# mLSTM output stage: the products over 128 rows of all heads ahead of those over 64 rows, and four vectors of a filler step in one row

## The chip, the core and the metric

The kernel runs on one core of a Trainium2 chip, as one launch. The metric is device time in microseconds (us). Inside the core five engines work on queues of their own: TensorE (PE: matrix products, with PEld for its weight loads), VectorE (DVE), ScalarE (ACT), GpSimd (POOL) and SyncE (SP, which issues most of the transfers). TensorE reads its weights from a part of its 128 x 128 array; a product over 64 rows uses the upper or the lower half of the rows, a product with 32 columns of weights uses a strip of 32 columns.

## The reference, cut to what matters

One layer: a token mixer (bidirectional mLSTM with 4 heads, and a convolution group), then a mixture of 64 experts. The change lies in the mLSTM outputs and in the adaLN rows that are made beside them. For each chunk of 128 tokens, each direction and head:

```python
s = jnp.einsum('bhctk,bhcsk->bhcts', qc, kc) * jnp.exp(log_d - m_t[..., None])
e_int = jnp.exp(a - m_t)
num = (jnp.einsum('bhcts,bhcsv->bhctv', s, vc)
       + e_int[..., None] * jnp.einsum('bhcvk,bhctk->bhctv', C_prev, qc))
den = jnp.sum(s, axis=-1) + e_int * jnp.einsum('bhck,bhctk->bhct', n_prev, qc)
h = num / jnp.maximum(jnp.abs(den), jnp.exp(-m_t))[..., None]
```

The first sum runs over the 128 tokens of the chunk, the second over the 64 features of a head (QK_DIM = 64). The values have 128 features, and a column of ones makes the denominators along with them (129 columns). The adaLN rows are `silu(c) @ w_ada + b_ada`.

## The kernel before, in words

After the front (projections, gates, states of the chunks) `outputs` (L590 to L718) runs over 8 chunks x of 128 tokens. For each chunk and each direction d it makes
- `decay` (L617): the logarithms of the weights in `pM` by two products (L620, L623), their exponentials `Dm` on ScalarE (L626);
- `scores` (L613): four products over 64 rows (heads 0 and 2 in the lower half of the rows, 1 and 3 in the upper) into `pQ`; `scaled` (L633, L636): the scaled queries `qs`; and `Dm` times the scores (L645);
- `sums` (L649): for each head a product over 128 rows, `Dm` with the values `va` (L654), and a product over 64 rows, `qs` with the state `C` of tile `cst` (L655), added up in `pN`. There is one buffer of `pN`, two banks of PSUM; head h is in bank h % 2;
- `divide` (L660 to L667): ScalarE copies `pN` to `hd`, VectorE divides; then `norm`, and `gate` with four transposes (L685).

`sums` is called 16 times, so it has 64 products over 128 rows and 64 over 64 rows. Chunk x + 1 is prepared while chunk x is summed.

Between these, `filler(2)` takes two steps of `ada` (L721) twice in every chunk, 32 steps in all. A step loads two tiles of 256 KB each (`wa2`, five buffers, L750) and makes four products with 32 columns of weights (L753) into four strips of `pa`. The first 16 steps also load and split the output projection's weights (`wor`, L759).

A product of L613, L654, L655 or L753 runs in two passes on TensorE and stands as x2 in the trace; one of L633 or L685 has one pass. A scheduler sets the order in which each engine gets its instructions: it takes what it holds ready, in the priority of the program, so filler products stand wherever it put them. After the stage come the output projection (L436 to L438), the router, and the experts, whose weights SyncE streams in (L1423).

```python
            for h, p in heads:
                o = pN[:, h % 2, h // 2, :DV + 1]
                mm(o, Dm[:, h % 2, h // 2], va[:, x + 2, h], start=True, stop=False)
                mm(o, qs[p, h // 2], C[p, h // 2], start=False, stop=True)
```

Of the kernel before, what the change touches and what calls it, by code (L numbers as in the profile page):

```python
# [32 lines left out]
class Layer:  # L33
# [19 lines left out]
    # ---------------------------------------------------------------- constants  # L53
# [51 lines left out]
    # ---------------------------------------------------------------- front  # L105
    def front(self, cp):
# [27 lines left out]
        # ---- adaLN: shift and scale of the mixer, features on partitions  # L134
# [12 lines left out]
        def squares(src, a, b):  # L147
            """Sums of squares over tiles of features, for tokens a to b."""
            for k in range(8):
                sq = vf[:, NT * (1 + k % 3):][:, :b - a] if k else vf[:, a:b]  # L150
                nc.scalar.activation(sq, src[:, k], AF.Square)
                if k:
                    nc.vector.tensor_tensor(vf[:, a:b], vf[:, a:b], sq, op=OP.add)
# [21 lines left out]
        def products(k):  # L175
            """Shift and gain of the features of tile k, the input's features summed in four parts."""
            p, n = (small, 1) if k % 3 == 2 else (wl, 2)
            w = p.tile([128, 8, 256], F32, name="wa1", bufs=n)
            self.wa1 = nc.sync.dma_start(w, A["wa1"][k]).ins
            a1 = pa[:, k % 2]  # L180
            for i in range(2):
                for n in range(4):
                    mm(a1[32 * n:32 * n + 32], cs[:, 2 * n + i], w[:, 2 * n + i], start=i == 0, stop=i == 1,
                       skip_group_check=True)
# [50 lines left out]
        # The first products go along with the features.  # L235
        U, Y = X[:, :4], X[:, 4:]
        first = [(f, j, pj.tile([128, 512], F32, name="pf", bufs=4)) for j in range(2) for f in (8, 4)]
        # The tensor engine's clock is up only after work: products that nobody reads until the sums are there.
# [47 lines left out]
        # ---- projections with features on partitions  # L286
# [41 lines left out]
        # ---- values and gates with tokens on partitions  # L328
# [80 lines left out]
    def behind(self, engine=mybir.EngineType.PE):  # L409
        """What follows runs behind what the engine has been given so far."""  # L410
        return self.tc.issue_after(next(i for i in reversed(self.nc.cur_bb.bb.instructions) if i.engine == engine))

    @contextmanager
    def later(self, n):
        """Lower priority for the scheduler: work that fills gaps."""
        tc = self.tc
        tc.cur_priority += n
        yield
        tc.cur_priority -= n
# [20 lines left out]
    # ---------------------------------------------------------------- mLSTM  # L440
    def gates(self, sp, pp, gt, colG, colF, colW, acol):
        """In steps: other products come between them."""
# [89 lines left out]
    def bound_rows(self, cp):  # L532
        """-M and exp(m - M) as rows of all heads, one for every direction and chunk: the high parts and, at partition
        64, the low ones."""
        nc = self.nc
        sp, sp_ = self.pool("rwt", 1)
        self.idr = cp.tile([80, 16], F32R, name="idr")
        idf = sp.tile([80, 16], F32, name="idf")
        nc.vector.memset(idf, 0.0)
        for h in range(2):  # L540
            nc.vector.tensor_copy(idf[64 * h:64 * h + 16], self.ident[64 * h:64 * h + 16, 64 * h:64 * h + 16])
        nc.vector.tensor_copy(self.idr, idf)
        out = []
        for i in range(2):
            raw = sp.tile([80, 2, 256], F32, name=f"rw{i}")
            nc.vector.memset(raw, 0.0)
            for d in range(2):
                v = self.rowd[i, BWD * d + 8:BWD * d + 40].rearrange("(c a s) t -> s c a t", a=2, s=2)
                for p in (8 * d, 64 + 8 * d):
                    for s in range(2):  # L550
                        nc.sync.dma_start(raw[p:p + 8, s].rearrange("p (a t) -> p a t", a=2), v[s])
            R = cp.tile([80, 2, 256], F32R, name=f"rwR{i}")
            nc.scalar.copy(R, raw)
            nc.vector.tensor_tensor(R[64:], raw[64:], R[64:].bitcast(F32), op=OP.subtract)
            out.append(R)
        self.close(sp_)
        return out

    def states(self, sp, pp, va, kT, cst, colW, acol):
        """The states before each latent chunk."""  # L560
# [29 lines left out]
    def outputs(self, qT, kT, va, cst, colG, colF, rows, os):  # L590
# [48 lines left out]
        def products(x, Dm):  # L639
            """The weights within the chunk and the scaled queries, both ways."""  # L640
# [8 lines left out]
        def sums(x, d, Dm, qs):  # L649
            pN = pp.tile([128, 2, 2, 256], F32, name="pN")  # L650
            C = cst[:, d, x if d == 0 else 7 - x]
            for h, p in heads:
                o = pN[:, h % 2, h // 2, :DV + 1]
                mm(o, Dm[:, h % 2, h // 2], va[:, x + 2, h], start=True, stop=False)  # L654
                mm(o, qs[p, h // 2], C[p, h // 2], start=False, stop=True)  # L655
# [64 lines left out]
    # ---------------------------------------------------------------- adaLN of the later stages  # L720
    def ada(self, pp):  # L721
        """Gates, shift and scale as rows in DRAM; row j is made at partitions 32 j .. 32 j + 31."""
# [21 lines left out]
        for step in range(32):  # L744
            n, k = divmod(step, 8)
            if k == 0:
                ps = pp.tile([128, 256], F32, name="pa")
            for h in range(2):
                w = ap.tile([128, 2, 256], F32, name="wa2", bufs=5)
                nc.sync.dma_start(w, A["wa2"][n, k, :, 2 * h:2 * h + 2])  # L750
                for i in range(2):
                    j = 2 * h + i
                    nc.tensor.matmul(ps[32 * j:32 * j + 32], self.csil[:, k, 0:1].to_broadcast([128, 32]), w[:, i],  # L753
                                     start=k == 0, stop=k == 7, skip_group_check=True)
# [78 lines left out]
def cut(r):  # L833
    """Blocks of the expert with rank r: (first half of its list, rows). Those of 64 or 32 rows take native products
    and come first."""
# [7 lines left out]
def schedule():  # L843
    """Order of the experts (by rank)."""
# [12 lines left out]
def table():  # L857
    """Blocks in their order: (number of the expert, first half of its list, rows, column in the tables of rows).
    The shared expert comes first and last; its blocks are token tiles."""
# [23 lines left out]
class Full(Layer):  # L883
# [72 lines left out]
    # ---------------------------------------------------------------- token mixer output, router  # L956
    def mixer_out(self, cp, X):
# [111 lines left out]
        def place(j, pl, mask, eq):  # L1069
            """Place of every assignment in its expert's list: half block and row. The row's one-hot carries the  # L1070
            token's index in two parts."""
# [64 lines left out]
    def rms_apply(self, tp, v, g, add, junk, t, out, nm, eng=None):  # L1136
        """out = v rsqrt(mean v^2) g + add."""
# [9 lines left out]
    # ---------------------------------------------------------------- lists of the experts' tokens  # L1147
    def ranks(self, rp, bank, first_r, first_c):
        """Tokens of every expert and its rank by them, with experts on partitions (twice)."""
# [15 lines left out]
    def lead(self, cp, rp, pp):  # L1165
        """Some experts with a middling number of tokens so far take the first ranks: their weights are loaded ahead of
        the lists."""
# [17 lines left out]
    def route(self, cp, rp, pp, pI):  # L1185
        """Token and destination of every row of the half blocks, in the order of the static schedule."""
# [35 lines left out]
        # rows of the sums in parts, for the blocks of 64 and 32 rows  # L1222
# [5 lines left out]
        # blocks behind the schedule  # L1228
# [15 lines left out]
    def spill(self):  # L1244
        """Blocks of experts that have more tokens than the static schedule holds."""
# [95 lines left out]
    def row_weight(self, junk, x, e, out):  # L1341
        """Weight of expert e (its number in every row) in the rows of x."""
# [4 lines left out]
    def compact(self, rp, sl, width, outs, eq):  # L1347
        """sl (128, 8, 64): the slot of every (token, expert); outs: [(values (128, 64), psum (128 slots, blocks))]."""
# [23 lines left out]
    # ---------------------------------------------------------------- experts  # L1372
# [19 lines left out]
    def bank(self, name, *shape):  # L1392
        """A bank of PSUM for one of the four stages, from the two pools in turn."""
# [5 lines left out]
    def unit(self, dt, free, since, n=NU, keep=0):  # L1399
        """The unit that has been free for the longest time, or none if no more than keep of them are."""  # L1400
# [64 lines left out]
    def mm6(self, out, x, w, k, nk, s):  # L1465
        """out += x @ w."""
# [5 lines left out]
    def stage_gu(self, x, w, rows=128, rw=None):  # L1472
        """A block of 64 rows has up and gate in the two halves of the partitions, one of 32 rows also the two halves
        of the sum over the features. The rows' weights go with up."""
# [48 lines left out]
    def stage_dn(self, hT, w, b):  # L1523
        """Output rows, in two or four parts on top of each other for a block of 64 or 32 rows."""
# [14 lines left out]
        else:  # L1539
            n = 1  # L1540
# [20 lines left out]
    def pipeline(self, experts):  # L1561
        """experts in order of first use; the shared one (None) comes first and last."""
# [66 lines left out]
        def row(key):  # L1629
            """Half of a unit that holds a tile until the end."""  # L1630
# [6 lines left out]
        def run(i0, i1):  # L1637
            """The blocks i0 .. i1 - 1, one stage of each behind another's."""
# [54 lines left out]
    # ---------------------------------------------------------------- shared expert, sum over the chosen experts  # L1693
# [90 lines left out]
def layout():  # L1784
    """Tables of the static schedule: they depend on the shapes alone."""
# [22 lines left out]
```

## Time and profile before

| | us |
|---|---|
| median of 3 runs | 1513.09 (1513.04 to 1519.22) |
| profiled execution, first to last instruction (span) | 1511.1 |
| TensorE busy in the span | 1442.5 (95%) |
| VectorE, ScalarE, GpSimd busy | 1130.7, 754.4, 469.9 |
| TensorE's mean granted clock | 0.99 of 2.4 GHz |
| mean transfer rate | 246 GB/s |

The output stage runs from 326 us to about 434 us in the span. A row of the timeline gives start, length, engine, line, operation, the tile written and the tiles read, the part of the array (rows * columns), the shape, and the number of merged instructions. The length of a row of products reaches to the end of its last product; the next row can begin earlier, so the time that a row costs is read from start to start.

### The profile page before, as it was taken

The page shows a single profiled execution, that of the slowest core. Times are in us where ns is not written, and L with a number is a line of the kernel's source. Part 1 is how long each engine was busy: PE and PEld are TensorE (multiplying, and loading weights), DVE is VectorE, ACT ScalarE, POOL GpSimd, SP SyncE. Part 2 cuts the span into 40 slices and gives each one's busy share as a digit, 9 for nine tenths or more (in the row PEclk, how much of TensorE's full clock was granted, in tenths as well). Part 3 has the DMA queues.
Part 4 walks back from the last instruction along what each step waited for, and adds up shares of the span by engine and source line. Part 5 has one row for each costly group of instructions (what it writes and reads, how often), then busy time and mean ns, then how long its engine had stood idle before and what let it go on. Part 6 is the DMA issues. An engine that isn't in the chain of part 4 may idle for free. (4 is left out here: it accounts for less than half of the span.)

```text
span 1511.1 us, 22956 instructions
## 1 busy us (share of the span) xinstructions
PE 1442.5 (95%) x8205; PEld 1096.4 (73%) x8211; DVE 1130.7 (75%) x1942; ACT 754.4 (50%) x1241; POOL 469.9 (31%) x306
## 2 busy tenths in 40 slices
PE   6997999999999999999999999999999999999975
PEld 4787987765567754776788888888777777777764
DVE  6899979765657887843588788888777877777636
ACT  4420021244424335644566667677666776676621
POOL 0341101202112332233333323333433444555324
PEclk9999999999999999999999999999999999999998
DMA  8420051036544367998799999999999999999975
GB/s 334 158 77 28 1 196 31 18 111 220 171 155 164 142 242 283 334 329 283 247 287 323 328 314 326 328 341 343 322 352 285 348 331 305 313 351 322 335 249 209
DMA packets 94385, 371.64 MB, mean 246 GB/s; under 512 B 18269, under 2 KB 26789, under 8 KB 67770
## 3 DMA queue, kind: packets, MB, share of 16 engines
q1 hardware_dynamic: 65946, 298.48, 52.9%
q0 software_dynamic: 26032, 70.19, 19.1%
q10 hardware_dynamic: 2288, 1.45, 0.4%
q8 instruction: 66, 1.08, 0.3%
q14 instruction: 53, 0.43, 0.1%
HBM read 322.38 MB, written 62.19 MB: 254 GB/s over the span
## 5 line engine op out<-in xcount | busy, mean ns | idle before, releaser
L51 DVE TENSOR_TENSOR u<-u,u 128x1024 fp32r<-128x1024 f32 x354 | 422.2, 1221 | 124.0 <-ACT u L50 94.4
L50 ACT CAST u<-u 128x1024 fp32r<-128x1024 f32 x354 | 361.4, 1052 | 107.7 <-PE pgu L438 41.5
L1556 POOL DMA_INDIRECT acc<-yb,dst x98 | 194.7, 1986 | 351.6 <-ACT hTH L50 118.5
L436 PE MATMUL pgu<-u,xH 128*128 128x512 f32 x608 | 246.1, 405 | 0.4
L437 PE MATMUL pgu<-u,xH 128*128 128x512 f32 x608 | 238.9, 393 | 0.0
L438 PE MATMUL pgu<-u,xL 128*128 128x512 f32 x608 | 238.1, 392 | 0.0
L1436 POOL DMA_INDIRECT xg<-hxd,tok x98 | 124.6, 1271 | 192.8 <-DVE rwj L1344 63.1
L431 DVE SCALAR_TENSOR_TENSOR X<-X,cw 128x912 f32<-128x912 f32 (+14 forms) x120 | 154.0, 1309 | 1.1
L436 PEld LDWEIGHTS pgu<-u,xH 128*128 128x128 f32 x608 | 114.5, 188 | 25.6 <-ACT u L50 2.6
L438 PEld LDWEIGHTS pgu<-u,xL 128*128 128x128 f32 x608 | 114.4, 188 | 24.8
L437 PEld LDWEIGHTS pgu<-u,xH 128*128 128x128 f32 x608 | 114.7, 189 | 21.6
L436 PE MATMUL py<-u,hTH 128*128 128x512 f32 x304 | 122.1, 402 | 0.5 <-ACT hTH L50 0.5
L437 PE MATMUL py<-u,hTH 128*128 128x512 f32 x304 | 119.8, 394 | 0.0
L438 PE MATMUL py<-u,hTL 128*128 128x512 f32 x304 | 118.6, 395 | 0.0
L436 PE MATMUL pf<-hH,wfH 128*128 128x512 f32 x256 | 103.5, 408 | 0.0
L51 DVE TENSOR_TENSOR xL<-px,xH 128x512 fp32r<-128x512 f32 x152 | 97.7, 683 | 7.4 <-ACT xH L50 7.0
L437 PE MATMUL pf<-hL,wfH 128*128 128x512 f32 x256 | 101.8, 398 | 0.7 <-DVE hL L226 0.7
L438 PE MATMUL pf<-hH,wfL 128*128 128x512 f32 x256 | 101.3, 396 | 0.0
L50 ACT CAST xH<-px 128x512 fp32r<-128x512 f32 x152 | 84.0, 593 | 13.8 <-PE pgu L437 7.8
L1548 DVE COPY yb<-py 128x512 f32<-128x512 f32 x75 | 51.6, 688 | 46.2 <-PE py L438 45.1
L1458 PE MATMUL px<-ident,xg 128*128 128x128 f32 x600 | 83.7, 274 | 0.9 <-DVE yb L1548 0.9
L1492 ACT ACTIVATE sgu<-pgu 128x256 f32<-128x256 f32 x79 | 30.5, 386 | 101.0 <-PE pgu L438 101.0
(431 smaller groups left out, 2549.5 us busy)
## 6 DMA issues: line engine op xcount, KB each, us to landing
u<-in_we_dram SPq DMA_DIRECT2D x192, 1024.0 KB
wa<-in_wa_dram SPq DMA_DIRECT2D x64, 256.0 KB
wa<-in_wa_dram SPq DMA_DIRECT2D x8, 1024.0 KB
wfr<-in_wf_dram SPq DMA_DIRECT2D x16, 512.0 KB
v<-acc SPq DMA_DIRECT2D x16, 512.0 KB
acc<-zero SPq DMA_DIRECT2D x13, 512.0 KB
u<-in_ws_dram SPq DMA_DIRECT2D x6, 1024.0 KB
X<-in_xT_dram SPq DMA_DIRECT2D x8, 512.0 KB
```

Source lines behind the costliest of these rows:

```text
L50: self.nc.scalar.copy(H, src)
L51: return (eng or self.nc.vector).tensor_tensor(L, src, H.bitcast(F32), op=OP.subtract).ins
L431: nc.vector.scalar_tensor_tensor(y[:, :, a:b], u[:, :, a + o:b + o], cw[:, i:i + 1], y[:, :, a:b], op0=OP.mult, op1=OP.add)
L436: mm(out, lH, rH, start=start, stop=False, skip_group_check=free)
L437: mm(out, lH, rL, start=False, stop=False, skip_group_check=free)
L438: mm(out, lL, rH, start=False, stop=stop, skip_group_check=free)
L1436: nc.gpsimd.indirect_dma_start(out=x[:n], out_offset=None, in_=self.hx, in_offset=bass.IndirectOffsetOnAxis(ap=self.tok[:n, c:c + 1], axis=0),
L1458: nc.tensor.transpose(pt[:, k], x[:, (4 * q + k) * 128:(4 * q + k) * 128 + 128], self.ident)
L1492: nc.scalar.activation(sg, pg[:, :DE], AF.Silu)
L1548: nc.vector.tensor_copy(y[:, 512:], py)
L1556: nc.gpsimd.indirect_dma_start(out=self.acc[b % NA].rearrange("r (n d) -> (r n) d", n=n), in_=y[:rows], in_offset=None, out_offset=bass.In ...
```

## The change

In `sums` the loop over the heads is cut in two: all four products over 128 rows first, then all four over 64 rows. Only the first product in each bank (heads 0 and 1) still has the start flag. In `ada` a step issues both of its loads first, then its four products.

```diff
@@ sums
             C = cst[:, d, x if d == 0 else 7 - x]
+
             for h, p in heads:
-                o = pN[:, h % 2, h // 2, :DV + 1]
-                mm(o, Dm[:, h % 2, h // 2], va[:, x + 2, h], start=True, stop=False)
-                mm(o, qs[p, h // 2], C[p, h // 2], start=False, stop=True)
+                mm(pN[:, h % 2, h // 2, :DV + 1], Dm[:, h % 2, h // 2], va[:, x + 2, h], start=h < 2, stop=False,
+                   skip_group_check=True)
+            for h, p in heads:
+                mm(pN[:, h % 2, h // 2, :DV + 1], qs[p, h // 2], C[p, h // 2], start=False, stop=True,
+                   skip_group_check=True)
             return pN
@@ ada
+            ws = []
             for h in range(2):
-                w = ap.tile([128, 2, 256], F32, name="wa2", bufs=5)
-                nc.sync.dma_start(w, A["wa2"][n, k, :, 2 * h:2 * h + 2])
-                for i in range(2):
-                    j = 2 * h + i
-                    nc.tensor.matmul(ps[32 * j:32 * j + 32], self.csil[:, k, 0:1].to_broadcast([128, 32]), w[:, i],
-                                     start=k == 0, stop=k == 7, skip_group_check=True)
+                ws.append(ap.tile([128, 2, 256], F32, name="wa2", bufs=5))
+                nc.sync.dma_start(ws[h], A["wa2"][n, k, :, 2 * h:2 * h + 2])
+            for j in range(4):
+                nc.tensor.matmul(ps[32 * j:32 * j + 32], self.csil[:, k, 0:1].to_broadcast([128, 32]),
+                                 ws[j // 2][:, j % 2], start=k == 0, stop=k == 7, skip_group_check=True)
```

The rest of the diff takes comments out. In the changed kernel the products over 64 rows are at L657, the fillers at L756, the transposes at L688.

The order on TensorE for the second direction of the first chunk, before (`pN<-va,Dm` are the products over 128 rows, `pN<-cst,qs` those over 64 rows, `pa` is a filler, `pQ` holds the scores and scaled queries of the next chunk):

```order
L753 MATMUL pa<-wa_2776,csil 32x256 x2
L613 MATMUL pQ<-qT,kT 128x128 x4
L633 MATMUL pQ<-rwR_2243,idr 128x256 x2
L654 MATMUL pN<-va,Dm_2701 128x129
L655 MATMUL pN<-cst,qs_2719 128x129
L654 MATMUL pN<-va,Dm_2701 128x129
L655 MATMUL pN<-cst,qs_2719 128x129
L654 MATMUL pN<-va,Dm_2701 128x129
L655 MATMUL pN<-cst,qs_2719 128x129
L654 MATMUL pN<-va,Dm_2701 128x129
L655 MATMUL pN<-cst,qs_2719 128x129
L753 MATMUL pa<-wa_2817,csil 32x256
```

The same place on TensorE in the changed kernel:

```order
L756 MATMUL pa<-wa_2774,csil 32x256 x2
L613 MATMUL pQ<-qT,kT 128x128 x4
L633 MATMUL pQ<-rwR_2243,idr 128x256 x2
L654 MATMUL pN<-va,Dm_2701 128x129 x4
L657 MATMUL pN<-cst,qs_2719 128x129 x4
L756 MATMUL pa<-wa_2817,csil 32x256
```

Eight changes between 128 and 64 rows have become two; the neighbours stand where they stood.

A place with fillers among the products, on TensorE, the second direction of the third chunk, before:

```order
L633 MATMUL pQ<-rwR_2243,idr 128x256 x2
L654 MATMUL pN<-va,Dm_2865 128x129
L655 MATMUL pN<-cst,qs_2923 128x129
L654 MATMUL pN<-va,Dm_2865 128x129
L753 MATMUL pa<-wa_3028,csil 32x256 x2
L655 MATMUL pN<-cst,qs_2923 128x129
L654 MATMUL pN<-va,Dm_2865 128x129
L753 MATMUL pa<-wa_3032,csil 32x256 x2
L655 MATMUL pN<-cst,qs_2923 128x129
L654 MATMUL pN<-va,Dm_2865 128x129
L655 MATMUL pN<-cst,qs_2923 128x129
L753 MATMUL pa<-wa_3080,csil 32x256
```

And in the changed kernel:

```order
L633 MATMUL pQ<-rwR_2243,idr 128x256 x2
L654 MATMUL pN<-va,Dm_2865 128x129 x3
L756 MATMUL pa<-wa_3028,csil 32x256 x2
L654 MATMUL pN<-va,Dm_2865 128x129
L657 MATMUL pN<-cst,qs_2923 128x129
L756 MATMUL pa<-wa_3030,csil 32x256 x2
L657 MATMUL pN<-cst,qs_2923 128x129 x3
L756 MATMUL pa<-wa_3080,csil 32x256
```

The fillers keep their places, counted in products, and still stand in two pairs with other work between; they now cut the runs of equal products.

## Rows read from the trace of the kernel before

**Rows 1.** The page's first line.

```profile
span 1511.1 us, 22956 instructions
```

**Rows 2.** Windows of the stage and of the experts: busy us per engine, clock, DMA.

```profile
331.00:375.00 44.00, 43.49 (x267) 25.94 (x268) 24.88 (x61) 21.03 (x71) 7.09 (x6) 1.00 0.70 237
375.00:431.00 56.00, 56.00 (x361) 33.37 (x365) 37.14 (x91) 21.30 (x73) 11.81 (x11) 1.00 0.56 181
1000.00:1200.00 200.00, 199.91 (x1080) 153.84 (x1079) 155.94 (x229) 135.10 (x198) 71.51 (x46) 1.00 0.97 330
```

**Rows 3.** Waits of TensorE from 325 to 436 us: total, times, longest.

```profile
PE pa L753 <- DMA wa<-in_wa_dram: 1.5, 2, 1.2
```

**Rows 4.** Timeline of TensorE, first chunk, second direction: start, length, what.

```profile
334.77 0.64 PE L753 MATMUL pa<-wa,csil 128*32 128x256 f32 x8
335.34 0.71 PE L613 MATMUL pQ<-qT,kT 64*128 64x128 f32 x8
335.98 0.50 PE L633 MATMUL pQ<-rwR,idr 80*128 80x256 f32 x2
...
336.64 0.49 PE L655 MATMUL pN<-cst,qs 64*128 64x129 f32 x2
337.06 0.49 PE L654 MATMUL pN<-va,Dm 128*128 128x129 f32 x2
...
340.11 0.50 PE L633 MATMUL pQ<-rwR,idr 80*128 80x256 f32 x2
```

**Rows 5.** Timeline of TensorE, third chunk: a single pass, a run, a filler.

```profile
358.73 0.28 PE L654 MATMUL pN<-va,Dm 128*128 128x129 f32 x1
...
361.15 0.50 PE L633 MATMUL pQ<-rwR,idr 80*128 80x256 f32 x2
361.49 0.39 PE L654 MATMUL pN<-va,Dm 128*128 128x129 f32 x2
361.81 0.49 PE L655 MATMUL pN<-cst,qs 64*128 64x129 f32 x2
...
362.64 0.63 PE L753 MATMUL pa<-wa,csil 128*32 128x256 f32 x4
363.20 0.49 PE L655 MATMUL pN<-cst,qs 64*128 64x129 f32 x2
```

**Rows 6.** Timeline of VectorE: scores times weights, first and sixth chunk.

```profile
337.57 0.69 DVE L645 TENSOR_TENSOR Dm<-Dm,pQ 128x512 f32<-128x512 f32 x1
...
406.50 0.69 DVE L645 TENSOR_TENSOR Dm<-Dm,pQ 128x512 f32<-128x512 f32 x1
```

**Rows 7.** Timeline of TensorE, sixth chunk: second pair of scaled-query products.

```profile
408.04 0.48 PE L633 MATMUL pQ<-rwR,idr 80*128 80x256 f32 x2
```

**Rows 8.** Timeline of ScalarE, fourth chunk: three exponentials behind a copy of the sums.

```profile
382.97 0.89 ACT L626 ACTIVATE Dm<-pM,colG 128x128 f32<-128x128 f32 x3
```

**Rows 9.** SyncE's queue from 325 to 436 us: what its loads waited for.

```profile
SPq L750 <- PE pa L753: 61.0, 32, 5.0
```

**Rows 10.** Windows right behind the stage: granted clock and transfer rate.

```profile
448.00:450.00 2.00, 2.00 (x6) 1.52 (x6) 0.00 (x0) 0.00 (x0) 0.00 (x0) 0.50 0.98 305
450.00:455.00 5.00, 5.00 (x21) 4.06 (x20) 3.96 (x5) 1.17 (x3) 0.56 (x1) 0.88 1.02 348
```

**Rows 11.** Timeline of TensorE behind the stage: output projection at two clocks.

```profile
446.99 0.47 PE L436 MATMUL po<-woH,fH 128*128 128x512 f32 x1 [1.12 <-issue]
...
448.17 0.63 PE L437 MATMUL po<-woL,fH 128*128 128x512 f32 x1
448.59 0.63 PE L438 MATMUL po<-woH,fL 128*128 128x512 f32 x1
...
452.33 0.40 PE L437 MATMUL po<-woL,fH 128*128 128x512 f32 x1
452.56 0.39 PE L438 MATMUL po<-woH,fL 128*128 128x512 f32 x1
```

**Rows 12.** SyncE's queue from 520 to 660 us: what the experts' loads waited for.

```profile
SPq L1423 <- DVE u L51: 24.5, 7, 8.7
```

## The prediction

> **What bounds the kernel now.** I began with the windows by stage. From 331 to 431 us TensorE is busy for 99.5 of 100 us, and VectorE for 24.88 + 37.14 = 62.0 us; the mean rate of the transfers falls from 237 GB/s to 181 [rows 2]. The waits say the same: in the whole stage TensorE waits twice for a load, 1.5 us in all [rows 3]. So TensorE ends last here. Busy is not the same as working, though, and the timeline shows what fills it. Products over 128 rows (L654) and over 64 rows (L655) alternate, and each takes 0.42 us from its start to the next one's: 336.64, 337.06 [rows 4]. Where a product over 128 rows stands behind others of that shape (L633 at 361.15, L654 at 361.49), it takes 361.81 - 361.49 = 0.32, and its row is 0.39 long in place of 0.49 [rows 5]: coming from another shape costs it 0.10. One pass of L654 is 0.28 long, so the two passes of the 0.39 row start 0.11 apart, and take 0.22 [rows 5]. Of the 0.42, the other 0.20 go into the change of shape: 0.10 for coming in and 0.10 for leaving.
>
> Products over 64 rows gain more. The four of the scores alternate between the lower and the upper half of the rows and take 335.98 - 335.34 = 0.64 us together [rows 4]. Four lone ones take 4 x 0.42. Two halves run side by side.
>
> **The change part by part.** No product is added or taken away. I counted the runs of equal shape on TensorE over the stage, in the order of each kernel: 88 runs over 128 rows, 74 over 64 rows and 48 of fillers before; 46, 31 and 48 now.
>
> *The 128-row runs.* 42 fewer, at 0.20 to 0.21 us each [rows 4, 5]: 8.6 us. A group that nothing cuts shows the same: four lone products take 4 x 0.42 = 1.68, a run of four takes 0.20 + 8 x 0.11 = 1.08.
>
> *The 64-row runs.* Before, all 64 stand alone: 64 x 0.415 = 26.6 us. Now 11 of the 16 groups are whole and 5 are cut into three and one by a filler or by L633. Heads 0 and 2 use one half of the rows and one bank, 1 and 3 the others, as the scores do, so a whole group is priced like the scores, 0.64; three still need two rounds, 0.64, and the one 0.415. 11 x 0.64 + 5 x 1.06 = 12.3 us. Less by 14.2 us.
>
> *The fillers.* Here the change does less than its words say. The 48 runs of fillers are of the same sizes before and now; the queues of VectorE, GpSimd and SyncE, with every load, hold the same instructions in the same order. A pair of fillers takes 363.20 - 362.64 = 0.56 us [rows 5], and two pairs in one run 335.34 - 334.77 = 0.57 [rows 4]: joining would gain 0.56 a time, but the order joins nothing. I take 0; either end would be a pair more or less joined, 0.6 us.
>
> TensorE has 8.6 + 14.2 = 22.8 us less to do. Three things can come late now.
>
> *VectorE.* In each of seven chunks the second pair of L633 waits until VectorE has read the scores (L645). That has slack now: 340.11 - 338.26 = 1.85 us in the first chunk [rows 4, 6], 408.04 - 407.19 = 0.85 in the sixth [rows 6, 7]; the others, read in the same way, are 2.43, 2.01, 1.37, 1.53 and 1.72. One call of `sums` stands ahead of it and shrinks by at most 8 x 0.417 = 3.34 less 1.08 + 0.64, which is 1.62. So 0.25 + 0.09 + 0.77 = 1.1 us come back as waits; bounds 0 and 5.4 (all seven like the worst). Queued behind that wait are the next fillers and products on TensorE, which wait for a load at most.
>
> *ScalarE.* Its queue differs at one place: the copy that frees `pN` in the fourth chunk now stands behind three more exponentials of 0.89 us together [rows 8]. The next `sums` waits for that copy. 0 to 0.9; I take 0.4, as fillers stand between.
>
> *Loads.* From 331 to 375 us 237 x 44 = 10.4 MB land [rows 2]. The products' part of the stage, 105 us from 326 to 431, loses 22.8, so by the same ratio the stretch shrinks to 44 x 82 / 105 = 34.4 us, which asks for 303 GB/s. Right behind the stage the core moves 348 [rows 10]. SyncE's loads waited 61.0 us for fillers to free a buffer [rows 9], so today's rate is held down by TensorE. Bounds: below 0, since a load issued earlier can also end the 1.5 us of today; above, if nothing but 237 GB/s is to be had, that stretch keeps 9.6 us. I take 1.5, near the row of 348.
>
> Behind the stage all is handed down: TensorE is busy 199.9 of 200 us among the experts, and the experts' loads wait for engines' work, for example 24.5 us for VectorE's splits [rows 2, 12].
>
> Sum: 22.8 - 1.1 - 0.4 - 1.5 = 19.8 us. The span of 1511.1 [rows 1] becomes 1491.3; the median of the runs is 2.0 above the span, so 1493.3.
>
> **A rule weighed against the rows.** L654 behind L633 at 361.49 uses the same rows of the array, and its two passes are 0.11 us apart [rows 5]; so the weights of a pass are loaded beside the pass ahead of it. The Trainium skill (TensorE: Matmul & The Clock Gate, The mechanism) says that a weight load overlaps with running products only where its row group is another one. By that rule every pass of the new 128-row runs would keep the distance that passes have behind a change of shape. The trace speaks against it; the rule's outcome is the second rival.
>
> **The rivals.**
> 1. *Another engine or the loads take TensorE's place.* For: the first 44 us would move 303 GB/s, and the thinnest slack is 0.85. Against: 348 is reached elsewhere, and VectorE's 62 us fit into some 80. With both upper ends, 22.8 - 5.4 - 0.9 - 9.6 = 6.9; halfway from 19.8 to that the gain is 13: 1500.
> 2. *Weight loads don't hide.* A pass takes 0.21 us (row length 0.49 less the 0.28 of one pass) [rows 4]. The four products then take 8 x 0.21 + 0.1 = 1.78 against 1.68, so the 8.6 turn into -1.6: gain 14.2 - 1.6 - 1.5 = 11.1: 1502.
> 3. *Nothing is handed down.* If the experts' stream of loads (330 GB/s in their windows [rows 2]) set the end from a point that the stage doesn't move, the time stays at 1513. Against: TensorE is just as full there, and the stream's waits end with engines' work [rows 12].
> 4. *Slower: the clock falls.* When TensorE waited 1.12 us ahead of 446.99, the granted clock fell to 0.50, 1.2 GHz in place of 2.4 [rows 10, 11], and a product of 512 columns went from 0.23 to 0.42 us [rows 11], 1.8 times as long. If the shorter stage brought new waits that keep the clock down, its 82 us would become up to 150. The point from which it decides: each us of the stage then costs 0.8 more, so with 25 of its us at half clock the gain is gone; with all 82 the time is 1493 + 66 = 1559. Against: only some 3 us of waits are added, in pieces under 1 us, and the clock was 1.00 in all windows of the stage [rows 2].
>
> **How the numbers follow.** My forecast has 0.80, with its own range of 1490 to 1497 (gain 16 to 23: the late terms at nothing, or at some 4 us more than taken). Rival 1 has 0.10, rival 2 has 0.03, rival 3 has 0.04, rival 4 has 0.03. To hold the time 8 times in 10 the range takes in half of rival 1: 1489 to 1500. Half a per cent, 7.6 us, is about what a measurement of this kernel tells from no change. The forecast and rivals 1 and 2 are beyond it: faster 0.93; same 0.04 (rival 3); slower 0.03 (rival 4).
>
> **What would show it.** In the new profile L654 and L657 should stand in runs of x8 passes; a run of 128-row products should take 1.1 us from start to start, a whole run of 64-row products 0.64, and the stage from its first `pM` at 326 us to the last product over 64 rows about 85 us in place of 105. In the windows VectorE's share rises from 62% to about 78%, the transfer rate of the first half to about 300 GB/s. TensorE's waits for `wa` should stay under 3 us, and those of L633 for VectorE near 1. It would be wrong if the 64-row runs took 4 x 0.42, if 128-row passes stood 0.21 apart, or if the experts began 20 us earlier and the end did not move.

## The result, and the profile after

The changed kernel takes 1497.38 us (median of 4 runs, 1496.50 to 1501.26). The kernel before took 1515.18 on the same chip in the same rounds (median of 4, 1513.04 to 1519.22). The ratio is 0.9888, 95% interval 0.9868 to 0.9908: faster by 1.1%. 1493.3 was forecast, in a range of 1489 to 1500.

The page's first line after the change (before: [rows 1]):

```profile
span 1496.1 us, 22962 instructions
```

The windows of the stage after (columns as in [rows 2]: window, its length, busy us of PE, PEld, DVE, ACT and POOL, granted clock, DMA share, GB/s):

```profile
331.00:375.00 44.00, 42.63 (x320) 25.57 (x320) 30.35 (x73) 26.23 (x87) 8.12 (x7) 1.00 0.86 289
375.00:405.00 30.00, 29.86 (x249) 17.95 (x249) 24.36 (x58) 15.09 (x48) 6.81 (x7) 1.00 0.67 217
405.00:416.00 11.00, 9.85 (x88) 5.88 (x86) 9.40 (x24) 4.35 (x19) 2.98 (x3) 1.00 0.74 245
```

TensorE still ends last, but no longer without gaps: 82.3 us of 85 busy. VectorE has 64.1 of the 85 us (75%), and the first 44 us move 289 GB/s where they moved 237 [rows 2]. The granted clock is 1.00 (2.4 GHz) throughout, so rival 4 did not come.

TensorE's timeline after, first chunk, second direction, the place of [rows 4]:

```profile
338.56 0.50 PE L633 MATMUL pQ<-rwR,idr 80*128 80x256 f32 x2
338.90 1.05 PE L654 MATMUL pN<-va,Dm 128*128 128x129 f32 x8
339.88 0.72 PE L657 MATMUL pN<-cst,qs 64*128 64x129 f32 x8
340.53 0.62 PE L756 MATMUL pa<-wa,csil 128*32 128x256 f32 x2
341.18 0.50 PE L633 MATMUL pQ<-rwR,idr 80*128 80x256 f32 x2
```

Four products over 128 rows take 339.88 - 338.90 = 0.98 us from start to start, the four over 64 rows 340.53 - 339.88 = 0.65. The third chunk, the place of [rows 5], where fillers cut the runs:

```profile
359.04 0.83 PE L654 MATMUL pN<-va,Dm 128*128 128x129 f32 x6
359.81 0.62 PE L756 MATMUL pa<-wa,csil 128*32 128x256 f32 x4
360.36 0.49 PE L654 MATMUL pN<-va,Dm 128*128 128x129 f32 x2
360.78 0.49 PE L657 MATMUL pN<-cst,qs 64*128 64x129 f32 x2
361.19 0.62 PE L756 MATMUL pa<-wa,csil 128*32 128x256 f32 x4
361.75 0.71 PE L657 MATMUL pN<-cst,qs 64*128 64x129 f32 x6
362.39 0.62 PE L756 MATMUL pa<-wa,csil 128*32 128x256 f32 x2
```

A lone product still takes 0.42 (360.36 to 360.78), and three 64-row products as long as four (361.75 to 362.39, 0.64).

What TensorE waits for from 325 to 425 us (total, times, longest; the waits for loads before are in [rows 3]):

```profile
PE pa L756 <- DMA wa<-in_wa_dram: 1.9, 3, 0.9
PE pM L620 <- ACT X L397: 0.8, 1, 0.8
PE pQ L633 <- DVE Dm L645: 0.5, 1, 0.5
```

The wait for ScalarE (L397), ahead of the first `pM`, is 0.8 us in the kernel before too. The wait for VectorE is the one new kind, in the sixth chunk, whose slack was the thinnest [rows 6, 7]. Behind the stage the experts fill TensorE as before: from 1000 to 1200 us it is busy for 199.95 of 200 us, at 325 GB/s, against 199.91 and 330 [rows 2].

To see where the time went, I split each span at the first decay product (L620, `pM`) and at the end of the last 64-row product, and gave each pass in between the time from its start to the next one's. In the profile of before, 6 of the 16 records of L620 are missing, and their 0.8 us count with the fillers; so the table has a second execution of each kernel beside it (from the last experiment below), and the terms are read from columns with all 16.

| us | before | before, again | after | after, again |
|---|---|---|---|---|
| up to the first `pM` | 325.9 | 328.0 | 330.2 | 332.1 |
| from there to the last 64-row product | 105.1 | 104.6 | 85.9 | 85.9 |
| of it, 64-row products | 26.62 | 26.63 | 12.38 | 12.38 |
| of it, 128-row products | 25.32 | 25.31 | 18.06 | 17.30 |
| of it, fillers | 29.48 | 28.17 | 30.54 | 30.24 |
| of it, all else | 23.6 | 24.4 | 24.8 | 25.9 |
| behind it | 1080.1 | 1077.9 | 1080.0 | 1080.8 |

The stage lost 18.6 to 19.2 us, and they arrive at the end: what lies behind takes 1077.9 to 1080.8 us in all four columns. But the front, which the change doesn't touch, was 4 us longer in both executions of the changed kernel.

### The profile page after: what moved, and what is told of

It is laid out like the page before. It is cut to its first block, busy times and chain, and to the rows that moved or that the text cites. A ratio compares the mean times of both kernels' runs of the same rounds, so it can differ in the third digit from the quotient of the medians.

```text
span 1496.1 us, 22962 instructions
## 1 busy us (share of the span) xinstructions
PE 1426.1 (95%) x8211; PEld 1088.5 (73%) x8211; DVE 1133.3 (76%) x1942; ACT 753.7 (50%) x1241; POOL 477.9 (32%) x306
## 3 DMA queue, kind: packets, MB, share of 16 engines
q0 software_dynamic: 26032, 70.19, 19.2%
q8 instruction: 66, 1.08, 0.3%
## 5 line engine op out<-in xcount | busy, mean ns | idle before, releaser
L51 POOL TENSOR_TENSOR wfL<-wfr,wfH 128x1024 fp32r<-128x1024 f32 x14 | 48.0, 3428 | 118.2 <-ACT wfH L50 104.2
```

The costliest lines, as they stand in the source:

```text
L51: return (eng or self.nc.vector).tensor_tensor(L, src, H.bitcast(F32), op=OP.subtract).ins
```

## The experiments

My theory: each change of shape costs TensorE 0.2 us, products over 64 rows in different halves run side by side, and the stage's gain is handed down in full. Each experiment was timed in rounds with the kernel before, whose median was 1514.67 us beside the first four, 1515.63 beside those with pairs and with two buffers, 1515.67 beside three buffers and the repeats, and 1514.18 beside the kept weights.

**Only the products regrouped** (the filler step as before).

```diff
-            ws = []
             for h in range(2):
-                ws.append(ap.tile([128, 2, 256], F32, name="wa2", bufs=5))
-                nc.sync.dma_start(ws[h], A["wa2"][n, k, :, 2 * h:2 * h + 2])
-            for j in range(4):
...
+                w = ap.tile([128, 2, 256], F32, name="wa2", bufs=5)
+                nc.sync.dma_start(w, A["wa2"][n, k, :, 2 * h:2 * h + 2])
+                for i in range(2):
...
```

> The regrouped products alone, with the filler step as it was before. If the whole gain comes from the regrouping (my theory), the time is that of the changed kernel, 1497 +- 3 us, and the stage from its first pM product to the last product over 64 rows takes 86 us (105.1 before, 85.9 in the changed kernel). If the filler edit carries a part, the stage is 88 us or longer.

1496.59 us, ratio 0.9878 (0.9852 to 0.9905); the stage takes 85.96 us, as in the changed kernel. The whole gain lies in `sums`.

**Only the filler step changed** (`sums` as before): that part of the diff on the kernel before.

> The filler edit alone on the kernel before. My theory: nothing, 1513 to 1517 us, the stage 105 us. If joining four vectors works on the chip although the order shows the same pairs, some 27 pairs of 0.56 us: up to 15 us less. Its profile also shows a second time when the stage begins: 326 us before and 330 in the changed kernel, with the same order ahead of it; if that is chance (the granted clock in the front), it lies anywhere between 326 and 332 here.

1515.97 us, ratio 1.0010 (0.9995 to 1.0025); stage 104.63 us, fillers in it 29.04 us. Issuing both loads ahead of four products changes nothing: in its trace every engine's instructions stand in the order of the kernel before.

**As many changes of shape, but no product right behind its own head's.** This tells the price of the shape from that of adding to the same place of `pN` twice running; the changed filler step is in it.

```diff
-            for h, p in heads:
-                mm(..., Dm..., va..., start=h < 2, stop=False, ...)
-            for h, p in heads:
-                mm(..., qs..., C..., start=False, stop=True, ...)
+            seen = []
+            for k, h in (("d", 0), ("c", 1), ("d", 2), ("c", 3), ("d", 1), ("c", 0), ("d", 3), ("c", 2)):
...
+                mm(pN[:, h % 2, h // 2, :DV + 1], l, r, start=len(seen) < 2, stop=h in seen, skip_group_check=True)
+                seen.append(h)
```

> The changed kernel with the products of a call in the order 128 rows head 0, 64 rows head 1, 128 rows head 2, 64 rows head 3, 128 rows head 1, 64 rows head 0, 128 rows head 3, 64 rows head 2: as many changes of shape as before (88 and 74 runs), but no product adds to what the product just ahead of it wrote. Theory of the shapes: no gain over the kernel before, 1513 to 1517 us, each product 0.42 us from start to start, stage 105 us. Rival: the 0.2 us are the wait of a product for the sum that the product ahead wrote in the same place of pN; then the stage falls to about 90 us and the time to 1499.

1516.47 us, ratio 1.0017 (0.9999 to 1.0036), stage 105.01 us. TensorE's timeline in it, second direction of the first chunk:

```profile
341.35 0.49 PE L657 MATMUL pN<-cst,qs 64*128 64x129 f32 x2
341.77 0.49 PE L657 MATMUL pN<-va,Dm 128*128 128x129 f32 x2
342.19 0.49 PE L657 MATMUL pN<-cst,qs 64*128 64x129 f32 x2
342.60 0.49 PE L657 MATMUL pN<-va,Dm 128*128 128x129 f32 x2
```

0.42 us for each, as before, though each adds to another head than the one ahead of it. The price is the change of shape. The Trainium skill (TensorEngine Tiling (Array Packing), Key Properties) says that changing the tiling mode drains TensorE, and gives no price; this trace agrees that such a change costs time, 0.2 us each; the draining itself no row shows.

**The 64-row products in another order**: heads 0 and 2, which use one half of the rows, next to each other, then 1 and 3.

```diff
-            for h, p in heads:
+            for h, p in (heads[0], heads[2], heads[1], heads[3]):
                 mm(pN[:, h % 2, h // 2, :DV + 1], qs[p, h // 2], C[p, h // 2], start=False, stop=True,
```

> The changed kernel with the four products over 64 rows in the order heads 0, 2, 1, 3, so that two of the same half of the rows follow each other, then two of the other; runs and changes of shape as in the changed kernel. If the halves run side by side, only heads 2 and 1 can: three rounds in place of two, a whole run takes 0.86 us in place of 0.64, 16 x 0.22 = 3.5 us more at most, about 1500 us. If the gain were the changes of shape alone, nothing changes: 1497.

1498.12 us, ratio 0.9903 (0.9872 to 0.9934), stage 86.02. I expected a run to become longer, and it did not:

```profile
339.40 1.06 PE L654 MATMUL pN<-va,Dm 128*128 128x129 f32 x8
340.39 0.72 PE L657 MATMUL pN<-cst,qs 64*128 64x129 f32 x8
341.04 0.62 PE L756 MATMUL pa<-wa,csil 128*32 128x256 f32 x2
```

The run takes 0.65 us in this order too. Passes still start in pairs (in this row at 340.387 and 340.400, then at 340.601 and 340.615). So the experiment doesn't separate side by side from one behind another, as it was meant to; the pairs of starts show side by side directly, for the two passes of one 64-row product stand 0.21 us apart when it is alone. The second of a pair starts 6 to 7 ns behind the first when the halves alternate, and 13 to 14 ns behind it in this order. What sets that distance was not tried.

**Two and two**: the heads in two pairs, 128-row products of a pair and then its 64-row products. Runs half as long, nothing else.

```diff
-            for h, p in heads:
-                mm(..., Dm..., va..., start=h < 2, stop=False, ...)
-            for h, p in heads:
-                mm(..., qs..., C..., start=False, stop=True, ...)
+            for two in (heads[:2], heads[2:]):
+                for h, p in two:
+                    mm(..., Dm..., va..., start=h < 2, stop=False, ...)
+                for h, p in two:
+                    mm(..., qs..., C..., start=False, stop=True, ...)
```

> The changed kernel with a call's products in two groups: 128 rows for heads 0 and 1, 64 rows for 0 and 1, then the same for 2 and 3. 58 and 46 runs in place of 46 and 31. By the prices of the prediction 12 more 128-row runs at 0.20 us and 16 calls with two runs of two at 0.42 in place of one of four at 0.64 make 2.4 + 3 = 5 us: stage 90 to 91 us, time 1502. If what counts is only that no product over 64 rows stands directly behind the one of its own head, nothing changes: 1497.

1501.52 us, ratio 0.9916 (0.9889 to 0.9942), stage 88.40. From its timeline (128-row products at L655, 64-row products at L658):

```profile
341.10 0.61 PE L655 MATMUL pN<-va,Dm 128*128 128x129 f32 x4
341.64 0.49 PE L658 MATMUL pN<-cst,qs 64*128 64x129 f32 x4
342.06 0.71 PE L655 MATMUL pN<-va,Dm 128*128 128x129 f32 x4
342.70 0.49 PE L658 MATMUL pN<-cst,qs 64*128 64x129 f32 x4
```

A pair over 64 rows takes 0.42 us (342.06 - 341.64), just what a lone one takes: the second is free. A pair over 128 rows takes 0.64 (342.70 - 342.06): 4 x 0.11 and 0.20 for the changes. So the products take some 5 us more than in the changed kernel, as expected, but the stage only 2.5 and not the 4 to 5 that I had for it: TensorE's waits for loads are 1.0 us here in place of 1.9, and that for VectorE is gone; the remainder is not broken down. The pairs bring 16.7 of the stage's 19.2 us.

**One load of 512 KB per filler step**, two buffers, so that four filler products become ready at once. If a change of shape costs 0.2 us wherever it is, fewer filler runs gain too. On the kernel before, then on the changed one:

```diff
-                w = ap.tile([128, 2, 256], F32, name="wa2", bufs=5)
-                nc.sync.dma_start(w, A["wa2"][n, k, :, 2 * h:2 * h + 2])
+            w = ap.tile([128, 4, 256], F32, name="wa2", bufs=2)
+            nc.sync.dma_start(w, A["wa2"][n, k])
+            for j in range(4):
...
```

> The same one load of 512 KB on the kernel before, with its products over 128 and 64 rows in turn: 80, 73 and 33 runs in place of 88, 74 and 48. If joining the fillers is worth the same without the regrouped products, the stage goes from 105 to about 95 us and the time from 1515 to 1505; if the loads eat it, the stage stays above 102.

1508.08 us, ratio 0.9954 (0.9932 to 0.9976), stage 94.55: the stage gains 10.5, with fillers at 17.56 us in place of 29.48. TensorE waits 1.2 us for filler weights, so in this longer stage such loads come in time.

> The changed kernel with one load of 512 KB in a filler step in place of two of 256 KB, in two buffers in place of five, so that all four vectors come free together. In its order the fillers stand in 33 runs, nearly all of four vectors, in place of 48; runs over 128 rows 39 (46), over 64 rows 34 (31). By the price of a pair, 0.56 us, 15 runs fewer are 8.4 us, the other runs about 1 more: the stage goes from 86 to 77 us and the time to 1488. Rival: with two buffers the fillers wait for their loads, TensorE's waits for wa grow from 1.9 us to 8 or more, and the stage stays at 84 or above.

1494.88 us, ratio 0.9880 (0.9858 to 0.9902), stage 82.19. The fillers cost 17.58 us here too, some 13 less than in the changed kernel, but the stage gained only 3.7. Waits of TensorE in it, 325 to 432 us:

```profile
PE pa L754 <- DMA wa<-in_wa_dram: 7.7, 11, 1.2
```

and its windows:

```profile
331.00:341.00 10.00, 8.77 (x61) 6.24 (x58) 4.72 (x11) 6.78 (x20) 0.00 (x0) 0.66 0.82 279
341.00:375.00 34.00, 31.46 (x280) 20.18 (x284) 30.41 (x73) 21.80 (x73) 7.75 (x7) 1.00 0.83 281
```

5.8 us more of waits for loads than in the changed kernel, and a granted clock of 0.66 in the first window: 6.8 of its 10 us at 1.2 GHz in place of 2.4. With 77 us expected, the waits alone make it 82.8, but this fits in part by chance. The fillers lost 13 us where 8.4 had been reckoned, and the lower clock took back up to 3 us (an estimate: 6.8 us, less 6.8 / 1.8 by the products of [rows 11]).

**The same with the fillers kept behind the products**: the scheduler may not put them ahead of what TensorE has been given.

```diff
-                filler(2)
+                with self.behind():
+                    filler(2)
```

> As the run with one load of 512 KB, and the products of each call of the fillers must stand behind the last product of the sums ahead of it: 42, 33 and 31 runs in place of 39, 34 and 33. By the price of a run about 0.6 us less than there, within what can be measured of it; 1487 to 1489 us. If the order of fillers against loads matters, the waits for wa differ by more than 2 us between the two.

1496.65 us, ratio 0.9888 (0.9866 to 0.9909), stage 81.74, waits for filler weights from 325 to 432 us 5.8 in place of 7.7. The stage is shorter by 0.45 us, about as expected; the waits differ by 1.9, just short of the 2 us that were to tell whether the order matters, and the median is far above the 1487 to 1489 that I expected. Only the profiled execution came near, at 1489.52, and its first `pM` came at 325.8 us.

**Three buffers.** Did the waits come from having two?

```diff
-            w = ap.tile([128, 4, 256], F32, name="wa2", bufs=2)
+            w = ap.tile([128, 4, 256], F32, name="wa2", bufs=3)
...
-                    raw = (wp if len(raws) < 15 else ap).tile([128, 512], F32, name="wor", tag="wo",
-                                                              bufs=32 if len(raws) < 15 else 1)
+                    raw = wp.tile([128, 512], F32, name="wor", tag="wo", bufs=32) if len(raws) < 15 else ap.tile(
+                        [128, 4, 256], F32, name="wa2", bufs=3)[:, :2].rearrange("p a b -> p (a b)")
```

> The changed kernel with one load of 512 KB per filler step, as in the run with two buffers of that size, but with three of them (the last tile of the output projection's weights takes one of the three for a while, so that they fit). The run with two buffers had its stage at 82.2 us, with 7.7 us of TensorE's waits in it for filler weights, against 1.9 us in the changed kernel. If the buffers set those waits (a load is issued only when the step two before is done), three take most of them: waits for filler weights under 3 us, stage 76 to 78 us, about 1489 us at a first decay product at 330 us. If the rate of the transfers sets them (about 280 GB/s in the first half, where no stretch of the stage had over 340), the waits stay at 6 to 8 us, the stage at 80 to 82 us, and the time at 1493 to 1495 us.

1494.67 us, ratio 0.9860 (0.9836 to 0.9885), stage 84.24. TensorE's waits from 325 to 432 us, then those of SyncE's queue from 325 to 415:

```profile
PE pa L754 <- DMA wa<-in_wa_dram: 7.6, 10, 1.7
```

```profile
SPq L752 <- PE pa L754: 26.6, 24, 3.7
SPq L752 <- DMA wa<-in_wa_dram: 25.7, 19, 2.1
```

The waits stay, so the buffers do not set them. SyncE's queue (SPq) itself stands 25.7 us behind earlier transfers of filler weights, which came to 1.6 us in the changed kernel. This is the best ratio of all, but its interval overlaps that of the changed kernel. Its stage is longer than with two buffers, and longer than the 80 to 82 us expected. Here too 6.8 us of the stage ran at 1.2 GHz, but as many did with two buffers, so the clock does not explain the difference, which stays open.

**Weights kept**: the filler weights of two steps serve all steps, and 60 of the 64 loads are gone.

```diff
+        raws, kept = [], []
...
-                ws.append(ap.tile([128, 2, 256], F32, name="wa2", bufs=5))
-                nc.sync.dma_start(ws[h], A["wa2"][n, k, :, 2 * h:2 * h + 2])
+                if step < 2:
+                    kept.append(ap.tile([128, 2, 256], F32, name=f"wk{len(kept)}"))
+                    nc.sync.dma_start(kept[-1], A["wa2"][n, k, :, 2 * h:2 * h + 2])
+            ws = kept[2 * (step % 2):2 * (step % 2) + 2]
```

> The changed kernel with the filler weights of the first two steps kept and used by all 32 steps: 60 of the 64 loads of 256 KB are left out, and the adaLN rows are made from the wrong weights. By the order the filler runs fall from 48 to 24, the runs over 128 rows from 22 to 18 and those over 64 rows from 21 to 17. If transfers are what ended the gain of the runs with one load per step (7.6 us of waits for filler weights with two and with three buffers), the waits for filler weights are gone here and the stage is 73 to 77 us (84.2 us of the run with three buffers, less 7.6 us, less up to 3 us for its fewer changes of shape), the time 1484 to 1488 us with a first decay product at 330 us. If another engine stands right behind (VectorE was busy for 78% of the stage there), waits for it take the place of the waits for loads and the stage stays at 80 us or above.

The stage takes 76.2 us, as the transfers' theory had it. TensorE's waits from 325 to 432 us, and the first window:

```profile
PE pQ L633 <- DVE Dm L645: 3.4, 5, 1.2
PE pN L654 <- ACT hd L663: 1.4, 3, 0.9
PE pa L757 <- DMA wk<-in_wa_dram: 1.1, 1, 1.1
```

```profile
331.00:375.00 44.00, 40.39 (x380) 27.15 (x381) 36.80 (x89) 28.45 (x93) 9.14 (x9) 1.00 0.37 119
```

Without the loads, VectorE's scores are what TensorE waits for. The whole time missed my expectation by far: 1577.49 us, ratio 1.0426 (1.0398 to 1.0453). Lines that the changed kernel never runs appear behind the stage (L1374, L1319); I take it that the wrong adaLN rows send the tokens to other experts, in blocks that don't fit the static schedule. Only its stage can be read.

**Both kernels once more**, for the front.

> The changed kernel once more, nothing edited. Theory: the 4 us by which the forecast was too low are mostly the front, whose length varies by some us from one execution to the next; the median over more executions should then stay at 1496 to 1498 us, and the kernel before in the same rounds at 1514 to 1516 us, the ratio at 0.988. Stage 85.5 to 86.5 us wherever it begins. Rival: the changed kernel's own front is longer; then its first decay product comes at 330 us again while the kernel before shows 326 us.

> The kernel before once more, nothing edited, for its profile. Theory: its first decay product at 326 us was an early one by chance; here it comes at 329 to 333 us, the stage is again 104.5 to 105.5 us and the remainder 1079 to 1081 us. Rival: the first decay product is at 326 us again, and the change moves the front by 4 us.

The changed kernel: 1500.29 us, ratio 0.9889 (0.9864 to 0.9915), first `pM` at 332.1 us, stage 85.93, behind it 1080.8. The kernel before, one execution: 1512.23 us, first `pM` at 328.0, stage 104.57, behind it 1077.9. The ratio repeats, but the median of the changed kernel lies 2.3 us above the top of what I expected, and this pair of profiles again has the front 4 us longer in the changed one. By the pair alone the rival stands. The other profiles speak against it. With only the filler step changed, every engine has the order of the kernel before, and the first `pM` comes at 332.5 us; with the fillers kept behind the products `sums` is regrouped, and it comes at 325.8. The windows from 20 to 35 us of the kernel before, of the changed one, and of these two, in this order, one fence each:

```profile
20.00:35.00 15.00, 13.95 (x115) 10.29 (x115) 10.69 (x22) 5.79 (x10) 2.04 (x2) 1.00 1.00 392
```

```profile
20.00:35.00 15.00, 13.90 (x96) 10.73 (x100) 8.60 (x17) 5.24 (x8) 2.96 (x2) 0.77 0.80 318
```

```profile
20.00:35.00 15.00, 13.93 (x82) 10.39 (x83) 7.42 (x16) 3.97 (x6) 2.96 (x2) 0.66 0.71 285
```

```profile
20.00:35.00 15.00, 14.06 (x114) 10.43 (x115) 10.70 (x22) 5.92 (x10) 2.04 (x2) 1.00 1.00 389
```

The front goes with this window's clock, with either `sums`. In the fourteen profiles the first `pM` comes at 325.8 to 328.6 us where the clock is 1.00 (four profiles, 381 to 397 GB/s), at 329.7 to 330.8 where it is 0.89 or 0.77 (seven, 293 to 364 GB/s), and at 332.1 to 332.5 where it is 0.66 (three, 282 to 286 GB/s); a clock between 0.50 and 1.00 is a mean of the two levels, 1.2 and 2.4 GHz. Whether the loads come late and the clock falls for it, or the other way round, was not tried and stays open, and so does whether an early front is rarer with the regrouped products.

## Why the prediction was right, and where it was off

**The 64-row runs, 14.2 us: right.** They fell from 26.63 to 12.38, 14.25 us. The crossed order shows that it is the shape; the run of pairs shows that the second of two halves is free.

**The 128-row runs, 8.6 us: nearly.** They fell from 25.31 to 17.30 in the second execution, 8.0 us. In the first it is 7.3, but 0.6 of the 18.06 is a wait for a load, which a reading from start to start gives to the product ahead of it:

```profile
412.82 0.49 PE L654 MATMUL pN<-va,Dm 128*128 128x129 f32 x2
413.91 0.62 PE L756 MATMUL pa<-wa,csil 128*32 128x256 f32 x4 [0.60 <-DMA wa<-in_wa_dram]
```

Of the 11 whole runs, three take the 1.09 us that I wrote (1.08) and eight 0.98, since these stand behind L623, L633 or L688, from which coming in costs nothing; that was so before too [rows 5]. I called L633 a product of the same shape, but it has 80 rows: not every change of shape has a price.

**The fillers, 0: right for the edit, not for the change.** By the edit alone they stood at 29.04 us against 29.48. In the changed kernel they take 2.1 to 2.4 us more than in the second profile of before. Of it, 1.5 to 1.6 us are loads that came late, and the other 0.5 to 0.7 is the wait of L633 for VectorE, which a reading from start to start gives to the filler ahead of it.

**What came late: 3.0 us were taken, some 3.5 came, in other shares.** The products lost 22.2 us (14.25 and 8.0), the stage 18.6 to 18.7. In TensorE's list of waits, loads have 1.9 and 1.8 us in the two profiles of the changed kernel, after 1.5 and 0.7 before. But that list holds idle time alone, and TensorE counts as busy with one pair of fillers while the next pair has no weights yet:

```profile
345.91 1.19 PE L756 MATMUL pa<-wa,csil 128*32 128x256 f32 x8
347.03 0.71 PE L613 MATMUL pQ<-qT,kT 64*128 64x128 f32 x8
```

```profile
346.47 0.14 PEld L756 LDWEIGHTS pa<-wa,csil 128*32 128x32 f32 x4 [0.42 <-DMA wa<-in_wa_dram]
```

The two pairs take 347.03 - 345.91 = 1.12 us, where two that are ready take 0.57 [rows 4]. Read in this way, from start to start, late loads cost 4.4 and 4.6 us in the two profiles of the changed kernel, after 1.9 and 1.4 before: 2.5 to 3.2 us more, about twice the 1.5 taken. VectorE's wait before L633 costs 0.7 and 0.5 us in place of 1.1, and none for ScalarE's copy shows in place of 0.4. One term was too small and two were too large, so that their sum came out near is luck. The rate of the first half rose to 289 GB/s, short of the 303 asked for.

**Handed down: right.** 1080.1 us behind the stage before, 1080.0 after (1077.9 and 1080.8 in the second profiles, so to within some 3 us); rival 3 falls. Rival 2 (weights of a pass are not loaded beside the pass ahead) falls with the run of 0.98 us: eight passes that use the same rows of the array stand 0.11 apart. By the rule of the Trainium skill that stood behind it (TensorE: Matmul & The Clock Gate, The mechanism: overlap only with another row group) they would stand as far apart as behind a change of shape; the measurement decides against it here. Rival 1 was right about what is next: late loads took back some 3 us here, and with some 13 us less of fillers the list of waits has 5.8 more.

**The base: off by 2 us, which is half of the miss.** I worked from one execution of 1511.1 us and three runs with a median of 1513.09. The kernel before had medians of 1514.2 to 1515.7 in the other groups. Its profiled execution had the early front, 325.9 us, and the changed kernel's had 330.2. Measured against runs of the same rounds the gain was 1515.18 - 1497.38 = 17.8 us, 2.0 under the 19.8; of that 0.6 to 1.2 is the stage. The rest goes with the granted clock of the whole runs. Runs of both kernels with the same mean clock, at each value from 0.983 to 0.987, are on the average 17.2 to 19.6 us apart, about the stage's 18.6 to 19.2; but the mean over all ten runs of the changed kernel is 0.985, over those of the kernel before 0.987. In the stage both have 1.00, so the difference lies outside it; whether it is chance is not shown. No step of the mechanism failed; the terms of what comes late were mis-sized, and the forecast should have carried the spread of the front, some 6 us, in its base.

## What to carry to other kernels

Read products from start to start: an engine that is busy for 99.5 of 100 us can still lose nearly a fifth of it to changes of shape, and can wait for loads without being idle; an order that keeps equal shapes together is worth the number of changes times their price (0.2 us here, and the whole second product where two halves of the rows run side by side). Before counting the gain of such an order, look at what the engine's queue really holds: the second half of this change altered the program's words and no queue. When the work on one engine shrinks, ask how much sooner its loads must come. For a stage 19 us shorter they came some 3 us late here; for fillers 13 us shorter on top, in loads of twice the size, the stage kept only 3.7 of the 13.

## What was not expected of the hardware

- The order of 64-row products within a run doesn't matter: with two of one half next to each other the run took the same 0.65 us, in pairs of starts 13 to 14 ns apart in place of 6 to 7.
- A third buffer of 512 KB left the waits for filler weights where they were (7.6 against 7.7 us), with 25.7 us of SyncE's queue spent behind earlier transfers. In the first 10 us of the stage the changed kernel moved 335 GB/s, so a rate of 285 is not the most that can be had; what holds those transfers back stays open.
- The front of one and the same kernel differs by some us from run to run, in step with its granted clock and its transfer rate in the first 35 us.
